# The same decoder layer, its instruction order made by the scheduler's timeline model instead of its default model

## The chip, the cores and the metric

The kernel runs on one core of one Trainium2 chip. A core has five engines that work at the same time, each from a queue of its own that it takes strictly in the order in which it was written: TensorE (PE in the profile; its weight loads are shown apart as PEld), VectorE (DVE), ScalarE (ACT), GpSimd (POOL) and SyncE (SP, which in this kernel issues nearly all the DMA transfers). An instruction that needs another engine's result waits for a semaphore, and everything behind it in its queue waits too. Data lies in a memory of 128 partitions that all engines reach (SBUF), and matmul sums in a small accumulator memory (PSUM). The metric is device microseconds (us) of one execution of the whole program.

## What is computed

One inference step of one decoder layer, for a prompt of 1024 tokens and eight samples of 8 tokens each (1088 tokens), with 1024 features, all in 32-bit floats.

```python
def decoder_layer(x, ...):
    x = x + 0.5 * rms_norm(swiglu_ffn(rms_norm(x, ffn1_norm_pre), ffn1_w_up, ffn1_w_down), ffn1_norm_post)
    m, ... = parallel_mixers(rms_norm(x, mix_norm_pre), w_in, ...)
    x = x + rms_norm(m, mix_norm_post)
    x = x + 0.5 * rms_norm(swiglu_ffn(rms_norm(x, ffn2_norm_pre), ffn2_w_up, ffn2_w_down), ffn2_norm_post)
    return x, ...

def parallel_mixers(h, ...):
    qa, ka, va, qkvb, zb, ab, bb, ga, gb = split_columns(h @ w_in)
    oa, ... = swa_prompt(qa, ka, va, attn_sinks)        # or swa_sample with a cache: window of 128
    xb, ... = causal_short_conv(qkvb, conv_buf, conv_w)
    ...
    ob, new_s = gated_delta_chunked(qb, kb, vb, g, beta, s0)
    ob = rms_norm(ob, dn_out_norm) * jax.nn.silu(zb)
    merged = jax.nn.sigmoid(ga) * (oa @ w_branch_a) + jax.nn.sigmoid(gb) * (ob @ w_branch_b)
    return merged @ w_out, ...

def step(s, xs):                                        # the delta net's scan over chunks, per head
    v_new = v_u_n - einsum(k_cum_n, s)
    o = einsum(q_dec_n, s) + einsum(qk_n, v_new)
    s = s * g_tot_n + einsum(k_dec_n, v_new)
    return s, o
```

A feed-forward block (FFN) has an inner width of 2816, that is 22 blocks of 128 gate and 128 up columns. The delta net has 4 heads; each solves a triangular system within its chunks and then runs the scan above.

## The kernel before

**Precision and weights.** A weight block is loaded by SyncE, split by ScalarE into a rounded high part (L111) and by VectorE into the low remainder (L112), and each product is three matmuls: high by high, high by low, low by high (`gemm`, L138 to L140; in the FFN's combined products L462 to L464; in its down projection L343 to L345). Tokens stand in three chunks of 384, 384 and 320 columns.

**Stages, in the order in which they are written.** First FFN (`FFN.run`): the third chunk takes its first groups of blocks (`pass_a`), then the first two chunks together by a scheme of seven products instead of eight (`two`, on sums and differences that `combine` makes, L264 to L272), then the rest of the third chunk. Norms (`rms`: squares on ScalarE, additions on VectorE at L168 and L171, a column sum by TensorE at L175) and residuals (`post`) are generators whose steps are handed out between the products. Then the mixers: projections for keys, values and queries (`do_kv`, `do_q`), the attention over the prompt and the samples, and for each of the four delta net heads the convolution projections (`conv_head`), a gate projection (`z_unit`) and `delta_head`, with the 16 gate projections (`gate_unit`, `gate_do`) written between and behind them. Then the two branch products (`br`), the output projection, and the second FFN in the manner of the first.

**`delta_head`** is a chain of small matmuls and VectorE and ScalarE steps: the norms of q and k (L1001), decay matrices and Gram products in two groups of four chunks (L1060 to L1087), the inverse of the diagonal 32x32 blocks with a round trip through DRAM (L1143 to L1155), the rest of the inverse (L1174 to L1198), the scan over eight chunks (L1217 to L1236), the samples' part (L1246 to L1270), and the output norm. Heads 0 and 2 use one set of buffers and the PSUM tag `ph`, heads 1 and 3 another set and `py`. The output goes to DRAM (`obd`) and is loaded and split again for the branch products.

**What sets the order.** The functions above only say what depends on what. When the block that holds the context closes, the tile library's scheduler plays the program through on a model of the machine. Whenever an engine of the model can take an instruction, it gives it the one of the highest priority among those whose inputs and buffers are ready there; priority is the order of writing, moved forward where the kernel says `high_priority(offset=...)`. The order that comes out is written into the engines' queues, with semaphores for the dependences, and the chip follows it. The kernel steers this by hand in a few places: the splits of weights and the evacuations of projections are moved forward by 20000 places (L110, L682 and others), column sums of two norms are kept behind two products that are ready (`behind`, L718), and the attention's matmuls of the two halves are chained in turn. Three PSUM banks (`pa`) take the products, two each `ph` and `py`, one `po` the norms; eight slots hold split weights (`wp`).

**Lines that the prediction speaks of**: L171 and L175 (a norm's last addition and its column sum), L198 (the first scaling of the input), L272 (the low part of a combination), L468 (adding a PSUM sum to an SBUF tile in `two`), L111 and L112 (weight splits), L176 (the reciprocal root behind a norm's sum), L1008, L1063, L1174, L1217 and L1001 in `delta_head`, and the branch products' matmuls (`oabh`, `h_br`).

## Time and profile before

| | us |
|---|---|
| median of three runs | 2462.98 |
| lowest and highest of them | 2456.78, 2473.88 |
| the profiled execution | 2454.17 |
| span from its first to its last instruction | 2452.4 |
| ACT busy in it | 1146.2 |
| mean granted TensorE clock | 0.991 |

The profile gives for each engine its busy time, and for each instruction what ended the idle time before it. In it L12 is line 12 of the kernel, and `out<-in` names the tiles written and read. A table of stretches gives for each stretch its length, then for each engine its busy time and number of instructions, then the granted clock as a share of the full one, the share of time the DMA engines were busy, and GB/s. The list of waits gives the total, the number and the longest. A matmul's record lasts longer than the time to the next start, since matmuls are pipelined, so busy time is not time at full rate.

The order of time of the main stages, by the lines seen in the trace: the first FFN from 6 to some 775 us, the mixers to some 1490, the branch and output projections to some 1680, the second FFN to the end.

### The profile page before, as it was taken

How to read it: one execution, taken by the hardware profiler on the slowest of the kernel's cores; microseconds unless marked ns; L12 is line 12 of the kernel's file. 1: busy time of each engine (PE TensorE's matmuls, PEld its weight loads, DVE VectorE, ACT ScalarE, POOL GpSimd, SP SyncE). 2: the span in 40 equal slices, each digit the busy share in tenths (PEclk: the TensorE clock that was granted, in tenths of full speed). 3: DMA queues.
4: the chain of work that ended last, by engine and by line, in shares of the span. 5: the costliest groups of instructions: out<-in, count | busy, mean ns of one | idle time of the engine just before them, and what ended most of it. 6: DMA issues, size and time to landing. Idle time of an engine off the chain costs nothing.

```text
span 2452.4 us, 39218 instructions
## 1 busy us (share of the span) xinstructions
PE 2396.3 (98%) x14654; PEld 2307.2 (94%) x14654; DVE 1752.0 (71%) x3550; ACT 1146.2 (47%) x2326; POOL 48.6 (2%) x36
## 2 busy tenths in 40 slices
PE   8999999999999999999999999999999999999997
PEld 7999999999998988798898889999999999999997
DVE  8887657757788577698796646655997576676677
ACT  7644423324465377644655333255754333233344
POOL 0000000000000000000101000000000000000000
PEclk9999999999999999999999999999999999999998
DMA  7332212213454301222222345435523122122453
GB/s 269 125 112 86 74 48 86 70 52 112 155 175 142 105 29 45 77 65 73 71 68 73 99 143 158 142 129 184 182 93 97 48 82 78 45 85 80 152 164 133
DMA packets 159759, 257.98 MB, mean 105 GB/s; under 512 B 34800, under 2 KB 65968, under 8 KB 159560
## 3 DMA queue, kind: packets, MB, share of 16 engines
q1 hardware_dynamic: 159568, 255.47, 32.4%
q8 instruction: 115, 1.88, 0.3%
q14 instruction: 76, 0.62, 0.1%
HBM read 219.43 MB, written 36.96 MB: 105 GB/s over the span
## 4 chain that ended last, share of the span: by engine, by line
PE 43%; DVE 6%; DMA 2%; ACT 1%; issue 1%; SPq 0%; DVEq 0%; ACTq 0%
PE pa L139 6%; PE pa L140 6%; PE pa L138 6%; PE pa L462 4%; PE pa L463 4%; PE pa L464 4%; PE py L344 2%; PE py L345 2%; PE ph L345 2%; PE ph L344 2%; PE ph L343 2%; PE py L343 2%; DMA q_c_a<-in_up_dram 1%; DVE s L1149 1%; DVE s L1143 1%
## 5 line engine op out<-in xcount | busy, mean ns | idle before, releaser
L463 PE MATMUL pa<-cl,h_c_s 128*128 128x384 f32 x704 | 236.4, 336 | 4.7 <-DVE cl L272 4.7
L462 PE MATMUL pa<-ch,h_c_s 128*128 128x384 f32 x704 | 237.4, 337 | 2.0 <-DVE t L468 1.4
L464 PE MATMUL pa<-ch,l_c_s 128*128 128x384 f32 x704 | 236.2, 336 | 0.0
L468 DVE TENSOR_TENSOR t<-pa,t 128x384 f32<-128x384 f32 x308 | 170.3, 554 | 83.6 <-PE pa L464 83.1
L462 PE MATMUL pa<-ch,h_c_a 128*128 128x384 f32 x528 | 176.8, 335 | 0.1
L464 PE MATMUL pa<-ch,l_c_a 128*128 128x384 f32 x528 | 176.6, 334 | 0.0
L463 PE MATMUL pa<-cl,h_c_a 128*128 128x384 f32 x528 | 176.5, 334 | 0.0
L111 ACT CAST h_c_a<-r_c_a 128x512 fp32r<-128x512 f32 x132 | 81.8, 619 | 129.8 <-PE pa L463 110.9
L462 PEld LDWEIGHTS pa<-ch,h_c_s 128*128 128x128 f32 x704 | 132.8, 189 | 5.6 <-DVE t L468 5.2
L463 PEld LDWEIGHTS pa<-cl,h_c_s 128*128 128x128 f32 x704 | 133.0, 189 | 4.9 <-DVE cl L272 4.9
L464 PEld LDWEIGHTS pa<-ch,l_c_s 128*128 128x128 f32 x704 | 132.9, 189 | 0.0
L111 ACT CAST h_c_s<-q_c_s 128x512 fp32r<-128x512 f32 x132 | 82.0, 621 | 107.1 <-PE pa L463 96.3
L139 PE MATMUL pa<-xbl,h_ga 128*128 128x384 f32 (+1 forms) x384 | 129.3, 337 | 0.0
L138 PE MATMUL pa<-xbh,h_ga 128*128 128x384 f32 (+1 forms) x384 | 128.7, 335 | 0.0
L140 PE MATMUL pa<-xbh,l_ga 128*128 128x384 f32 (+1 forms) x384 | 128.4, 334 | 0.0
L462 PEld LDWEIGHTS pa<-ch,h_c_a 128*128 128x128 f32 x528 | 99.1, 188 | 0.8 <-DVE t L468 0.6
L463 PEld LDWEIGHTS pa<-cl,h_c_a 128*128 128x128 f32 x528 | 99.1, 188 | 0.0
L464 PEld LDWEIGHTS pa<-ch,l_c_a 128*128 128x128 f32 x528 | 99.1, 188 | 0.0
L138 PE MATMUL pa<-xbh,h_qkv 128*128 128x384 f32 (+1 forms) x288 | 96.7, 336 | 0.0
L139 PE MATMUL pa<-xbl,h_qkv 128*128 128x384 f32 (+1 forms) x288 | 96.6, 335 | 0.0
L140 PE MATMUL pa<-xbh,l_qkv 128*128 128x384 f32 (+1 forms) x288 | 96.3, 334 | 0.0
L111 ACT CAST h_c_s<-r_c_s 128x512 fp32r<-128x512 f32 x44 | 27.4, 623 | 146.4 <-PE pa L463 130.6
(603 smaller groups left out, 7438.4 us busy)
## 6 DMA issues: line engine op xcount, KB each, us to landing
r_c_a<-in_up_dram SPq DMA_DIRECT2D x132, 256.0 KB
q_c_a<-in_up_dram SPq DMA_DIRECT2D x44, 256.0 KB
q_ub<-in_up_dram SPq DMA_DIRECT2D x44, 256.0 KB
r_ub<-in_up_dram SPq DMA_DIRECT2D x44, 256.0 KB
r_ua<-in_up_dram SPq DMA_DIRECT2D x42, 256.0 KB
q_ua<-in_up_dram SPq DMA_DIRECT2D x42, 256.0 KB
r_da<-in_dn_dram SPq DMA_DIRECT2D x40, 256.0 KB
q_da<-in_dn_dram SPq DMA_DIRECT2D x40, 256.0 KB
```

The lines of the kernel that those rows point to most:

```text
L111: nc.scalar.copy(hi, full)
L138: nc.tensor.matmul(ps[:, :n], hi[:, j, :], at(xh, k), start=first, stop=False)
L139: nc.tensor.matmul(ps[:, :n], hi[:, j, :], at(xl, k), start=False, stop=False)
L140: mm = nc.tensor.matmul(ps[:, :n], lo[:, j, :], at(xh, k), start=False, stop=last)
L343: nc.tensor.matmul(ps[:, :n], hi[:, i, :], hh, start=i == 0, stop=False)
L344: nc.tensor.matmul(ps[:, :n], hi[:, i, :], hl, start=False, stop=False)
L345: nc.tensor.matmul(ps[:, :n], lo[:, i, :], hh, start=False, stop=i == len(hs) - 1)
L462: nc.tensor.matmul(ps, wh[:, k, :], xh[:, k, :], start=k == 0, stop=False)
L463: nc.tensor.matmul(ps, wh[:, k, :], xl[:, k, :], start=False, stop=False)
L464: nc.tensor.matmul(ps, wl[:, k, :], xh[:, k, :], start=False, stop=k == 3)
L468: nc.vector.tensor_tensor(out=out, in0=ps, in1=other, op=ALU.add)
L1143: nc.vector.tensor_tensor(out=tv, in0=Md[:, j + 1 :, j : j + 1].to_broadcast([34, m, j + 1]), in1=Ld[:, j : j + 1, 0 : j + 1].to_broadcast ...
```

## The change

The context that schedules the program is made with one more argument:

```diff
-    with _tile.TileContext(nc) as tc:
+    with _tile.TileContext(nc, schedule_with_timeline_sim=True) as tc:
         body(tc, d)
```

With it the scheduler plays the program through on another model of the machine: a timeline on which every instruction is a sequence of steps (decoding, waiting, holding an engine, taking effect, telling others), with queues of bounded length in front of the engines and a model of TensorE's clock. The default model has its own durations and no such steps. The rule by which an instruction is chosen, the priorities, the dependences laid by hand, the tiles and the instructions themselves are the same in both. What differs is at which moment of the model an engine is free and an input is ready, and so which instruction is chosen, and so the order within each engine's queue.

## The prediction

> **What bounds the kernel now.** I read the page's busy times first, then a table of the span cut into seven stages, then the list of what TensorE waited for, then the order of time around its longest waits.
>
> ```profile
> span 2452.4 us, 39218 instructions
> PE 2396.3 (98%) x14654; PEld 2307.2 (94%) x14654; DVE 1752.0 (71%) x3550; ACT 1146.2 (47%) x2326; POOL 48.6 (2%) x36
> ```
> ```profile
> core 0: us, PE busy (x) PEld busy (x) DVE busy (x) ACT busy (x) POOL busy (x), PEclk, DMA share, GB/s
> 0.00:100.00 100.00, 90.34 (x573) 85.96 (x574) 82.25 (x151) 74.27 (x150) 0.20 (x4) 1.00 0.65 221
> 100.00:700.00 600.00, 599.00 (x3522) 596.52 (x3521) 428.87 (x751) 240.29 (x450) 0.00 (x0) 1.00 0.29 92
> 700.00:1500.00 800.00, 778.52 (x4972) 702.64 (x4971) 579.60 (x1482) 432.45 (x970) 48.42 (x32) 0.99 0.29 91
> 1500.00:1700.00 200.00, 200.00 (x1230) 199.12 (x1230) 110.92 (x199) 78.79 (x154) 0.00 (x0) 1.00 0.41 134
> 1700.00:1900.00 200.00, 192.63 (x1197) 190.18 (x1197) 176.36 (x295) 114.16 (x223) 0.00 (x0) 0.98 0.42 139
> 1900.00:2400.00 500.00, 499.58 (x2935) 498.04 (x2935) 336.66 (x599) 187.80 (x347) 0.00 (x0) 1.00 0.30 96
> 2400.00:2452.40 52.40, 36.21 (x237) 34.74 (x235) 37.37 (x77) 18.40 (x36) 0.00 (x0) 0.86 0.29 102
> ```
>
> TensorE is the bound: it is busy for 2396.3 of 2452.4 us, and its 14654 matmuls stay what they are. A new order can touch only the 56.1 us in which it is idle, time that a busy record hides, and the clock. By stage the idle time is 9.66 us at the start, 1.00 in the first feed-forward block, 21.48 in the mixers (700 to 1500), 0 and 7.37 around the entry to the second feed-forward block, 0.42 in its body and 16.19 at the end. The two long feed-forward stages have nothing to win and a great deal to lose; the mixers and the entry at 1800 are where an order was badly guessed.
>
> ```profile
> PE po L175 <- DVE rms L171: 8.7, 4, 3.6
> PE pa L138 <- ACT xuh L198: 6.0, 1, 6.0
> PE pa L463 <- DVE cl L272: 4.7, 1, 4.7
> ...
> PE py L1174 <- DMA s<-bd: 2.1, 1, 2.1
> ```
> ```profile
> 774.08 0.33 PE L139 MATMUL pa<-xbl,h_k 128*128 128x384 f32 x1
> 774.25 0.34 PE L140 MATMUL pa<-xbh,l_k 128*128 128x384 f32 x1
> 777.56 0.91 PE L175 MATMUL po<-rms,eye 128*128 128x384 f32 x2 [2.97 <-DVE rms L171]
> ...
> 781.29 0.69 PE L138 MATMUL pa<-xbh,h_kvq 128*128 128x384 f32 x1
> ```
>
> The second fence is the kind of thing that a better model should mend. The column sums of the norm (L175) were placed in TensorE's stream ahead of the query projections (L138, h_kvq), as if the norm's additions on VectorE were done by then. They came 2.97 us late, and products that don't need that norm's sums stood behind them in the queue.
>
> ```profile
> 1018.00:1027.80 9.80, 6.08 (x49) 4.97 (x48) 8.67 (x24) 4.61 (x12) 2.55 (x2) 1.00 0.15 40
> ...
> 1341.90:1345.30 3.40, 3.40 (x26) 3.10 (x25) 1.67 (x6) 0.61 (x4) 1.16 (x1) 1.00 0.23 72
> 1798.00:1806.10 8.10, 5.21 (x34) 4.91 (x32) 8.10 (x10) 6.02 (x15) 0.00 (x0) 1.00 0.26 72
> ```
> ```profile
> 778.70:785.50 6.80, 5.86 (x16) 4.42 (x17) 4.53 (x10) 2.58 (x6) 0.00 (x0) 0.50 0.06 21
> 1027.80:1034.70 6.90, 6.90 (x24) 5.30 (x23) 3.97 (x11) 2.68 (x6) 0.39 (x2) 0.51 0.14 20
> 1178.00:1181.40 3.40, 3.40 (x13) 3.40 (x12) 1.46 (x10) 3.36 (x4) 0.00 (x0) 0.50 0.06 8
> 1345.30:1348.70 3.40, 3.40 (x11) 2.46 (x9) 2.62 (x7) 1.29 (x2) 0.74 (x1) 0.50 0.73 240
> 1806.10:1812.90 6.80, 5.02 (x16) 5.02 (x17) 5.69 (x8) 3.09 (x7) 0.00 (x0) 0.50 0.06 24
> ```
>
> These are two tables of short stretches, with the columns of the stage table; the last column but two is the granted clock. After each thin stretch of TensorE the clock is 0.50 for 3.4 to 6.9 us, so a gap is paid twice. TensorE is busy for 24.58 us of these five stretches (5.86 + 6.90 + 3.40 + 3.40 + 5.02); at full clock that work takes half, so 12.3 us are lost.
>
> **The change, part by part.** No instruction is added or removed: 14654 matmuls, 3550 VectorE, 2326 ScalarE and 36 GpSimd operations, and all DMAs stay, with their buffers and dependences. What moves is the place of each of them in its engine's queue, SyncE's DMA issues and GpSimd's included.
>
> *What an order could win at most.* Idle time in the mixers and the entry at 1800 is 21.48 + 7.37 = 28.9 us; with the clock's 12.3 that is 41.1 us. The start isn't counted: its 9.66 us hold the 6.0 us before the first matmul, while the first transfers land. Nor is the end: the last norm is a chain with no other work left.
>
> *What of it a better order can reach.* Two stretches have VectorE itself full: 8.10 of 8.10 us before 1806 and 8.67 of 9.80 before 1028. There TensorE's idle time (4.7 us in front of L463, and 9.80 - 6.08 = 3.72 us in the other) and half of the slow clock behind it ((5.02 + 6.90) / 2 = 5.96) are VectorE's work, 14.4 us that I leave. The other 26.7 us are latencies that ready products could cover. I take three quarters of them, 20 us, since transfers such as the 2.1 us in front of L1174 will still be guessed wrongly in places.
>
> [...]
>
> *What a new order can cost.* Three prices, each from both sides. (a) Evacuations on VectorE:
>
> ```profile
> L468 DVE TENSOR_TENSOR t<-pa,t 128x384 f32<-128x384 f32 x308 | 170.3, 554 | 83.6 <-PE pa L464 83.1
> ```
>
> Sums of the feed-forward blocks are taken out of three PSUM banks by L468 in 0.554 us each. VectorE waits 83.1 us for TensorE there, and TensorE is idle for 1.00 and 0.42 us in the two long stages, so the banks cover the delay now. A product is 12 matmuls, 0.17 us apart (774.08 and 774.25 above are two starts), some 2.1 us; two further banks cover two products, 4.2 us, less the 0.554 itself. An evacuation placed more than about 3.6 us late costs time. At best this gives back those 1.4 us; at worst one product's time (2.1 us) is lost in each of the 44 blocks, 92 us. I take nothing, as VectorE is busy for 428.87 of 600 us there. (b) The order of transfers: only 2.1 us of TensorE's waits end on one; bounds -2.1 and a few times that; I take nothing. (c) ScalarE's table loads:
>
> ```profile
> L176 ACT ACT_TABLE_LOAD x13 | 16.7, 1283 | 0.2
> ```
>
> An order that alternates functions more often pays 1.283 us of ScalarE each. ScalarE is busy for 432.45 of 800 us in the mixers, which covers it except in a norm's chain; taken as nothing, with 13 at most either way (16.7 us) as the bound.
>
> *Sum.* 2454.17 us is the profiled execution (2452.4 of span and 1.8 around it); less 20 it is 2434. It lies 8.8 us under the median of the runs shown, 2462.98 us, so on that footing I expect **2443 us**, 0.8% less.
>
> **The rivals.** *All of it goes:* also VectorE's share, 41 us, 2422 us. For it speaks that the order of VectorE's own three 1.75 us pieces before L463 is free; against it, that these 8.10 us were full.
>
> *Nothing net:* new waits of the same size come instead, 2463 us. For it: the feed-forward stages and 1500 to 1700, 1300 us together, have 1.4 us of idle time, so the present order is already good. An order that comes out nearly the same belongs here.
>
> *Slower, by the delta net's chain.*
>
> ```profile
> 1016.94 1.16 PE L1063 MATMUL ph<-s,s 128*128 128x128 f32 x8 [0.55 <-DVE s L1008]
> ...
> 1437.09 2.31 PE py L1001 x6
> ...
> L138 PEld LDWEIGHTS pa<-oabh,h_br x192: 187/188/188, 1488.4 to 1582.7; 128*128 128x128 f32 x192
> ```
> ```profile
> 1410.72 0.49 PE L1217 MATMUL py<-s,s 128*128 128x128 f32 x2
> ...
> 1412.85 0.47 PE L1217 MATMUL py<-s,s 128*128 128x128 f32 x2
> ```
>
> The four heads run from 1017 to 1439 us as one dependent chain, with projections put between its steps. The branch products (h_br) need the last head and start at 1488.4. In the 49 us between, that output is stored, loaded and split: 24 pieces (by the code, three chunks of eight) of some 0.55 us on VectorE, as in L468's row, are 13 us, and two transfers of a little over the 2.1 us of L1174's wait make some 19. So the chain may grow by about 30 us, 7% of its 422, before TensorE runs out of projections. One chunk step takes 2.1 us (two starts of L1217) and holds two hops. If the new model puts three more matmuls of 0.17 us (0.52 us) ahead of each hop, a head with some 36 hops (16 in its chunk loop, about 20 by the code) grows by 19 us, four by 75, and 45 us are exposed: 2508 us. Each further matmul per hop adds 25 us. Against it: a model whose times are right puts a chain step in as soon as its input is there.
>
> **How the numbers follow.** About 1% (24.6 us) is what a measurement of this kernel can tell from no change: faster is under 2438, slower over 2488. Most waits shrink: 0.42, of which 0.22 under 2438 (own range 2425 to 2458). All of it goes: 0.12, faster. Nothing net: 0.18, same. The chain is exposed: 0.28, slower. So faster 0.34, same 0.38, slower 0.28. The range runs from 2418, just past the case of all 41 us, to 2520, which takes in one chain case of 45 us and leaves the worse ones, about 0.12, out.
>
> **What would show it.** Right: no wait of some 3 us before L175 near 780; idle time of the 700 to 1500 stage near 8 us instead of 21.5; slow-clock stretches only behind VectorE-full windows; 1900 to 2400 as full as now. Wrong: TensorE waiting on L468 in the feed-forward stages; a last head that ends later than 1470 with TensorE idle before h_br; many more table loads than 13 in L176; a start or an end that is longer than 9.66 and 16.19 us of idle time.

## The result and the profile after

| | before | after |
|---|---|---|
| median, us | 2459.98 | 2531.99 |
| lowest and highest, us | 2456.78, 2473.88 | 2526.56, 2535.47 |
| profiled execution and its span, us | 2454.17, 2452.4 | 2532.87, 2531.2 |
| mean granted TensorE clock | 0.991 | 0.972 |

The medians are of four runs each; a fourth run of the kernel before moved its median from the 2462.98 us shown above. The change makes the kernel slower: the ratio of the times is 1.028, with a 95% interval from 1.0235 to 1.0325. The table of stages of the changed kernel, with the columns that it had before:

```profile
core 0: us, PE busy (x) PEld busy (x) DVE busy (x) ACT busy (x) POOL busy (x), PEclk, DMA share, GB/s
0.00:100.00 100.00, 83.15 (x515) 78.93 (x516) 74.95 (x141) 69.97 (x140) 0.20 (x4) 0.97 0.62 207
100.00:700.00 600.00, 600.00 (x3541) 599.73 (x3540) 428.41 (x752) 240.80 (x449) 0.00 (x0) 1.00 0.30 93
700.00:1500.00 800.00, 740.27 (x4655) 675.98 (x4655) 543.90 (x1412) 399.84 (x905) 41.29 (x28) 0.95 0.24 75
1500.00:1700.00 200.00, 185.29 (x1076) 174.07 (x1075) 114.11 (x203) 73.69 (x144) 9.88 (x4) 0.92 0.48 152
1700.00:1900.00 200.00, 197.15 (x1237) 194.27 (x1236) 146.05 (x246) 113.59 (x230) 0.00 (x0) 0.99 0.42 141
1900.00:2400.00 500.00, 500.00 (x2886) 500.00 (x2885) 347.63 (x622) 187.13 (x347) 0.00 (x0) 1.00 0.27 84
2400.00:2531.20 131.20, 114.94 (x756) 113.20 (x754) 93.51 (x179) 57.93 (x110) 0.00 (x0) 0.94 0.46 157
```

The span is 78.8 us longer. TensorE's idle time went from 56.1 to 110.4 us (+54.3). Its busy time went from 2396.28 to 2420.80 us (+24.5) for the same 14654 matmuls, at a mean clock of 0.972 instead of 0.991. The two make the 78.8 us.

By stage, idle time from 700 to 1700 went from 21.48 to 59.73 + 14.71 = 74.4 us (+53.0). The first 100 us have 7.2 more. The stretch at 1700 to 1900 has 4.5 less, and the two long feed-forward stages have none left. From its first matmul to the end the second feed-forward block took 2452.4 - 1679.4 = 773.0 us before and 2531.2 - 1766.0 = 765.2 after. So the loss lies in the mixers and at the entry to the branch products that follow them, and one gain of some 8 us lies behind them.

Within the mixers, three stretches of TensorE stand out (same columns):

```profile
1004.00:1043.00 39.00, 23.30 (x157) 13.92 (x155) 18.24 (x53) 25.91 (x57) 0.00 (x0) 0.72 0.23 81
...
1184.00:1240.00 56.00, 45.35 (x261) 36.03 (x261) 22.88 (x63) 22.73 (x59) 2.90 (x2) 0.74 0.14 39
...
1540.00:1580.00 40.00, 27.02 (x86) 19.79 (x87) 17.68 (x27) 12.84 (x24) 4.84 (x3) 0.62 0.51 164
```

They are idle for 15.7, 10.7 and 13.0 us, at clocks of 0.72, 0.74 and 0.62. In each of them the chain runs with hardly a projection between its steps: at the end of attention, where heads 0 and 1 run their chunk loops side by side, and at the end of head 3 with the entry to the branch products. The instruction rows of the heads' first matmul, the last gate product, and the chain's end with the entry to the branch products in time order:

```profile
L1063 PEld LDWEIGHTS ph<-s,s x32: 186/192/338, 1042.9 to 1294.7; 128*128 128x128 f32 x32
```
```profile
L139 PE MATMUL pa<-xbl,h_ga x384: 302/334/740, 1091.5 to 1536.7; 128*128 128x384 f32 x128, 128*128 128x320 f32 x64
```
```profile
1557.03 3.67 PE L1001 MATMUL py<-s,eye 128*128 128x512 f32 x6
1565.48 0.69 PE L138 MATMUL pa<-oabh,h_br 128*128 128x384 f32 x1 [4.78 <-ACT oabh L191]
1569.58 0.69 PE L139 MATMUL pa<-oabl,h_br 128*128 128x384 f32 x1 [3.42 <-DVE oabl L192]
```

The heads start at 1042.9 instead of 1017 (+26) and end at 1560.7 instead of 1439.4 (+121), so their 422 us have become 518. The gates are used up at 1536.7, 24 us before the chain ends; before the change they lasted for 49 us behind it. The branch products start 77 us later (1565.5 instead of 1488.5). Of the 121 us, then, 44 went into the cover that was there, and 77 show. At their entry TensorE waits again, for the pieces of `oab`, and the second feed-forward block starts 1766.0 - 1679.4 = 86.6 us later, so the branch and output products lose a further 9.6 us.

How a step gets later can be read in the chunk loop, here from one product of L1217 to the next step of the chain, L1224; first head 3 before the change, then head 2 after it (start, duration, operation):

```profile
1410.97 0.40 PE L139 MATMUL pa<-xbl,h_ga 128*128 128x320 f32 x1
...
1411.78 0.34 PE L138 MATMUL pa<-xbh,h_ga 128*128 128x384 f32 x1
1411.95 0.49 PE L1224 MATMUL py<-s,s 128*128 128x128 f32 x2
```
```profile
1437.70 0.49 PE L1217 MATMUL ph<-s,s 128*128 128x128 f32 x2
1437.94 0.42 PE L140 MATMUL pa<-xbh,l_ga 128*128 128x384 f32 x1
...
1441.58 0.31 PE L139 MATMUL pa<-xbl,h_ga 128*128 128x320 f32 x1
1441.73 0.38 PE L1224 MATMUL ph<-s,s 128*128 128x128 f32 x2
```

Before, 6 gate matmuls stand between them and the hop takes 1.2 us; after, 24 do and it takes 4.0. What L1224 waits for last is ScalarE's copy, whose rows in the two cases are:

```profile
1411.63 0.27 ACT L1223 COPY s<-py 128x128 f32<-128x128 f32 x1 [0.58 <-DVE s L1221]
```
```profile
1438.61 0.27 ACT L1223 COPY s<-ph 128x128 f32<-128x128 f32 x1 [0.58 <-DVE s L1221]
```

Before, L1224 starts 0.05 us after the copy's end; after, 2.85 us, all of them filled with gate matmuls. Over the 32 steps of the four chunk loops the time from the copy's end to L1224 went from 0.05 to 1.55 us at the median, while the other two lags of the step stayed under 0.1 us (from TensorE to VectorE, and from VectorE to ScalarE). The waits in front of L1174, which needs a head's blocks, grew as well, from 2.1 us (the engine's tile, what it waits for, us in total, times, longest):

```profile
PE ph L1174 <- DMA s<-bd: 9.1, 2, 5.6
PE py L1174 <- DMA s<-bd: 6.9, 2, 5.2
```

In the written order of TensorE's queue the runs of projections between other work of the mixers went from 4 to 13 matmuls at the median.

### The profile page after: what moved, and what is told of

It is laid out like the page before. It is cut to its first block, busy times and chain, and to the rows that moved or that the text cites. A ratio compares the mean times of both kernels' runs of the same rounds, so it can differ in the third digit from the quotient of the medians.

```text
span 2531.2 us, 39119 instructions
## 1 busy us (share of the span) xinstructions
PE 2420.8 (96%) x14654; PEld 2336.2 (92%) x14654; DVE 1748.6 (69%) x3550; ACT 1142.9 (45%) x2324; POOL 51.4 (2%) x36
## 4 chain that ended last, share of the span: by engine, by line
PE 84%; DVE 7%; DMA 3%; ACT 2%; issue 1%; SPq 0%; DVEq 0%; ACTq 0%
PE pa L139 10%; PE pa L138 10%; PE pa L140 10%; PE pa L462 8%; PE pa L464 8%; PE pa L463 8%; PE ph L343 3%; PE py L345 3%; PE ph L344 3%; PE py L343 3%; PE py L344 3%; PE ph L345 3%; DMA bd<-s 1%; DMA s<-bd 1%; DVE t L965 1%
## 5 line engine op out<-in xcount | busy, mean ns | idle before, releaser
L462 PE MATMUL pa<-ch,h_c_s 128*128 128x384 f32 x704 | 235.7, 335 | 0.0
L463 PE MATMUL pa<-cl,h_c_s 128*128 128x384 f32 x704 | 235.3, 334 | 0.0
L468 DVE TENSOR_TENSOR t<-pa,t 128x384 f32<-128x384 f32 x308 | 166.5, 552 | 82.2 <-PE pa L464 80.8
L462 PE MATMUL pa<-ch,h_c_a 128*128 128x384 f32 x528 | 177.1, 335 | 1.8 <-ACT t L380 1.8
L463 PE MATMUL pa<-cl,h_c_a 128*128 128x384 f32 x528 | 177.1, 335 | 0.0
L462 PEld LDWEIGHTS pa<-ch,h_c_s 128*128 128x128 f32 x704 | 132.3, 188 | 0.1
L463 PEld LDWEIGHTS pa<-cl,h_c_s 128*128 128x128 f32 x704 | 132.2, 188 | 0.0
L138 PE MATMUL pa<-xbh,h_ga 128*128 128x384 f32 (+1 forms) x384 | 129.4, 337 | 0.1
L140 PE MATMUL pa<-xbh,l_ga 128*128 128x384 f32 (+1 forms) x384 | 128.2, 334 | 0.0
L462 PEld LDWEIGHTS pa<-ch,h_c_a 128*128 128x128 f32 x528 | 99.4, 188 | 2.0 <-ACT t L380 2.0
L463 PEld LDWEIGHTS pa<-cl,h_c_a 128*128 128x128 f32 x528 | 99.5, 188 | 0.0
L140 PE MATMUL pa<-xbh,l_qkv 128*128 128x384 f32 (+1 forms) x288 | 96.6, 335 | 0.0
L138 PE MATMUL pa<-xbh,h_qkv 128*128 128x384 f32 (+1 forms) x288 | 95.9, 333 | 0.0
L112 DVE TENSOR_TENSOR l_c_s<-q_c_s,h_c_s 128x512 fp32r<-128x512 f32 x132 | 90.5, 687 | 0.3 <-ACT h_c_s L111 0.2
```

The costliest lines, as they stand in the source:

```text
L112: nc.vector.tensor_tensor(out=lo, in0=full, in1=f32(hi), op=ALU.subtract)
L138: nc.tensor.matmul(ps[:, :n], hi[:, j, :], at(xh, k), start=first, stop=False)
L140: mm = nc.tensor.matmul(ps[:, :n], lo[:, j, :], at(xh, k), start=False, stop=last)
L462: nc.tensor.matmul(ps, wh[:, k, :], xh[:, k, :], start=k == 0, stop=False)
L463: nc.tensor.matmul(ps, wh[:, k, :], xl[:, k, :], start=False, stop=False)
L468: nc.vector.tensor_tensor(out=out, in0=ps, in1=other, op=ALU.add)
```

## The experiments

The runs are called e1 to e18, and stand here by the question that they answer. Most of them hold one or more engines to the order that the other model gave them, by edges that only order, within the mixers (from L631 to the end of the gates). Both orders are made from the same program:

```diff
+    order = trace(BASE, None)[2]
+    nc, feed, _ = trace(FLAG, order)
...
+        for name, eng in order:
...
+            if eng.split(".")[1] in PIN[stage]:
+                if eng in last:
+                    tc.add_manual_dep(ins[k], last[eng], dep, reason="the other model's order")
+                last[eng] = name
```

In all of them the work is the same. The kernel before, timed beside them, had medians from 2458.05 to 2460.23 us.

### One engine's order at a time

```diff
+BASE, FLAG, PIN = False, True, ((), ('PE',), (), ())
```


> The timeline model makes the order, but within the mixers (from the sum at 631 to the end of the delta net) TensorE alone is held to the order that the default model gave it; VectorE, ScalarE, SyncE and GpSimd are free. Theory A, TensorE's order is the cause (it puts runs of 13 projection matmuls, at the median, between two steps of a chain instead of 4, the chain gets longer and the projections run out): the mixers get back nearly all of their 79 us; heads 0 to 3 take 420 to 440 us instead of 517; about 2455 us. Theory B, the order on VectorE and ScalarE stretches the chain: heads stay above 490 us; 2510 to 2535. Theory C, the order of transfers on SyncE (the waits in front of L1174 grew from 2.1 to 16 us): as B.

e1: 2498.74 us, ratio 1.0154 (1.0126 to 1.0183): 33 of the 72 us come back, between what A and B expected. The heads take some 465 us. The first row of TensorE's waits, and the rows of head 2's substitution loop on VectorE (count, shortest/median/longest in ns, first and last start), before and in this run:

```profile
PE ph L1174 <- DMA s<-bd: 21.7, 2, 19.9
```
```profile
L1143 DVE TENSOR_TENSOR s<-s,s x31: 169/356/2337, 1242.3 to 1288.9; 34x31 f32<-34x31 f32 x2, 34x60 f32<-34x60 f32 x2, 34x87 f32<-34x87 f32 x2, 34x112 f32<-34x112 f32 x2
```
```profile
L1143 DVE TENSOR_TENSOR s<-s,s x31: 183/366/2091, 1269.4 to 1337.3; 34x31 f32<-34x31 f32 x2, 34x60 f32<-34x60 f32 x2, 34x87 f32<-34x87 f32 x2, 34x112 f32<-34x112 f32 x2
```

L1174 waits for the blocks that this loop makes, by way of a transfer. The loop's 62 dependent operations take 22 us by themselves in both; the loop lasts 47.3 us before and 68.3 here, as 121 other operations (55.2 us, their records overlapping in part) stand between its steps instead of 92 (36.8 us); the counts of 135 and 106 in the expectation of e15 take in waits on semaphores. VectorE does to this chain what TensorE does to the other.

```diff
+BASE, FLAG, PIN = True, False, ((), ('PE',), (), ())
```


> The reverse: the default model makes the order, but TensorE is held in the mixers to the order that the timeline model gave it. Theory A: the loss appears, heads take about 515 us and the time is 2460 + 77 = about 2537 us. Theory B (VectorE and ScalarE) and C (transfers): 2455 to 2480, heads below 450 us.

e2: 2555.98 us, ratio 1.0398 (1.0365 to 1.0432): 24 us more than the change itself. TensorE's order is enough for the loss. That the other engines don't fit it is one reading of the further 24 us; e7 below, where they do, still takes 2548.55 us, so most of it isn't explained.

```diff
+BASE, FLAG, PIN = False, True, ((), ('DVE', 'Activation'), (), ())
```


> The timeline model makes the order, but VectorE and ScalarE are held in the mixers to the default model's order; TensorE's order is the timeline model's own, given those. Theory A: no gain, 2520 to 2550 us, since TensorE still takes projections in long runs. Theory B: the mixers get their 79 us back, about 2455 us. Theory C: about 2530.

e3: 2593.82 us in a single run, worse than all others and outside every expectation. TensorE, in the timeline model's own order for these fixed ones, takes projections in runs of 20 at the median. Theory B falls. It doesn't show that these two orders are harmless, since they fit another order of TensorE.

```diff
+BASE, FLAG, PIN = False, True, ((), ('PE', 'SP'), (), ())
```


> As e1, but TensorE and SyncE's transfers are held in the mixers to the default model's order, VectorE and ScalarE are free. Theory A2: within 10 us of the 2499 us with TensorE alone. Theory C: 2455 to 2470 us, the heads back to 425 us.

e6: 2540.69 us, ratio 1.0337 (1.0316 to 1.0358): 42 us worse than e1, not better. TensorE waits 43.0 us at L1174 and 11.0 us for the cache of keys (L910). Theory C falls, and A2's time is missed too. My reading, which no run separates, is that a transfer held to an old place waits for work that now comes later.

### Engines together

```diff
+BASE, FLAG, PIN = False, True, ((), ('PE', 'DVE', 'Activation'), (), ())
```


> As e1, but in the mixers TensorE, VectorE and ScalarE are all held to the default model's order; the transfers on SyncE and GpSimd's work stay in the timeline model's order. Held on TensorE alone, the heads took 465 us and the run 2499 us. Theory A2, the loss belongs to the orders of the three compute engines together (one that fits the other): heads near 425 us, 2450 to 2465 us (the first block's 8 us more and the second's 8 less cancel). Theory C, the other half is the order of the transfers: it stays within 10 us of 2499.

e5: 2457.13 us, ratio 0.9994 (0.9982 to 1.0005). The whole loss is gone, with the transfers in the timeline model's order. The row of the mixers' stage is nearly that of before (778.52 busy, clock 0.99):

```profile
700.00:1500.00 800.00, 777.07 (x4988) 702.26 (x4987) 579.03 (x1489) 436.32 (x979) 49.19 (x32) 0.99 0.29 92
```

The reverse in the default model's run:

```diff
+BASE, FLAG, PIN = True, False, ((), ('PE', 'DVE', 'Activation'), (), ())
```


> As e2 (2556 us, 18 more than the loss it was to reproduce), but the default model's run is held in the mixers to the timeline model's order on TensorE, VectorE and ScalarE. Theory A2: the timeline model's loss without the misfit between the engines, 2460 + 79 = about 2539 us, heads near 517 us. Theory C: below 2510, since the transfers go in the default order.

e7: 2548.55 us in a single run; the heads take 522 us. These three orders make the whole loss, and some 10 us more than A2 expected, with the transfers in the default order.

```diff
+BASE, FLAG, PIN = False, True, ((), ('PE', 'DVE'), (), ())
```


> As e1 (TensorE held in the mixers to the default order: 2499 us, with a wait of 19.9 us in front of L1174 for a head's blocks, whose substitution loop on VectorE took 68.3 us instead of 47.3), with VectorE held too; ScalarE free. Theory V, the other half of the loss is VectorE's order: the loop is back near 47 us, the wait near 2, and the time within 8 us of the 2457 us that all three engines gave. Theory S, it is ScalarE's: 2485 to 2500 us.

e16: 2473.45 us, ratio 1.0051 (1.0034 to 1.0069). The loop and the wait (2.5 us at most) came out as V expected, the time didn't: it is 16 us above the run with all three engines, where 8 were allowed. Head 2's loop is back:

```profile
L1143 DVE TENSOR_TENSOR s<-s,s x31: 179/358/2342, 1255.9 to 1303.8; 34x31 f32<-34x31 f32 x2, 34x60 f32<-34x60 f32 x2, 34x87 f32<-34x87 f32 x2, 34x112 f32<-34x112 f32 x2
```

```diff
+BASE, FLAG, PIN = False, True, ((), ('PE', 'Activation'), (), ())
```


> As e1, with ScalarE held too; VectorE free. Theory V: 2485 to 2500 us, the loop of head 2 above 60 us. Theory S: 2450 to 2465 us.

e17: 2496.52 us, ratio 1.0153 (1.013 to 1.0176), with the loop at 67.9 us and a wait of 18.1 us at L1174. So of the mixers' loss TensorE's order gives back 33 us and VectorE's 25 more; ScalarE's gives 16 once both are right and 2 when VectorE's is not. The shares depend on the order in which they are taken: with ScalarE's in place, VectorE's gives 39.

### Which part of the mixers

The same edges, in a part of their own that begins with the first head's convolution:

```diff
+    attention_sample(); MARK.append(len(list(nc.cur_bb.bb.instructions)))
+BASE, FLAG, PIN = False, True, ((), (), ('PE', 'DVE', 'Activation'), (), ())
```

> The timeline model, with TensorE, VectorE and ScalarE held to the default model's order from the first head's convolution to the end of the gates; attention, and what stands before it, in the timeline model's order. Theory A2: attention and the start of the heads keep their 26 us (1017 to 1043), the heads' and the overrun's 51 us come back: 2475 to 2490 us. If attention's delay is only a consequence of what the heads' projections do: 2455 to 2465.

e11: 2475.29 us, ratio 1.0061 (1.0039 to 1.0084), as A2 expected. The heads start at 1042.7 us and take 431 us. Heads and gates are 57 of the 75 us between the change and e5, attention and what stands before it the other 18.

### Is it a choice, and is it the projections' place?

```diff
-    attention_prompt()
+    with tc.high_priority(offset=10000): attention_prompt()
```
(and so for `attention_sample` and the four calls of `delta_head`)

> The timeline model, with a priority over the projections for all of attention and of the four heads. Theory A, with runs of projections that are taken while no step of the chain is ready by the model's times: a priority decides only between instructions that are ready at the same moment, so the runs stay (median 12 or 13 matmuls) and so does the time, 2515 to 2545 us. Rival D, the model has both ready and chooses the projections: the runs fall to about 4 and the time to 2450 to 2470.

e8: 2527.55 us in a single run, runs of 12 at the median. A priority hardly changes anything, which speaks for a model that takes a projection where it has no step of the chain ready.

```diff
+        if name not in FILL:
+            step = name
+        elif step and step != last and at[step] < at[name]:
+            tc.add_manual_dep(ins[at[name]], step, dep, reason="no earlier than in the default order")
```


> The timeline model, with one rule: in attention and the heads no projection matmul may stand ahead of the chain step that it stood behind in the default model's order; chain steps and all other engines are free. Theory A, projections spent too early are TensorE's part of the loss: most of the 33 us that the whole TensorE order gave back in e1 come back, 2495 to 2508 us. If it was the order of the chain steps among themselves: 2522 or more.

e14: 2514.74 us, ratio 1.0224 (1.0199 to 1.0249): 17 us, half of what the whole order of TensorE gave and between the two expectations. The heads take 480 us instead of 518, and 252 gate matmuls are left behind the last step, so the cover is kept. But from 700 to 1500 us TensorE is idle for 64.8 us (59.7 in the changed kernel): with the projections held back, the waits of the chain are bare. Projections spent too early are thus not the whole of TensorE's part.

```diff
+        j == 0 and turns and tc.add_manual_dep(st.ins, turns[-1], NOSYNC, reason="heads in turn")
```


> The timeline model, with one rule: on VectorE the first step of a head's substitution loop (62 dependent operations, L1143 and L1149) stands behind the last of the head before. In the timeline model's run heads 0 and 1 share VectorE step by step, 1083.4 to 1178.3 us for both, where the default order finished head 0's at 1095.5 and head 1's at 1155.3; both heads then reach TensorE together and the projections that need a head's buffers aren't there. Theory G, this sharing is a cause of its own: head 0's loop takes 40 to 52 us and ends by 1140, its chunk loop starts some 30 us earlier than 1183.7, TensorE's idle time of 10.7 us at 1184 to 1240 and the half clock there go, 2500 to 2518 us. Theory H, only TensorE's runs of projections matter: 2525 to 2540.

e13: 2524.72 us, ratio 1.0267 (1.0237 to 1.0296), outside both ranges by a little. The expectation misread the trace: the one stretch of 94.9 us for both heads was taken for a step-by-step sharing. Row by row, head 0's loop ends near 1143 and head 1's begins at 1137, so only four steps of each overlap. The 7 us lie at the edge of the runs' spread. Theory G falls with its premise: there was hardly any sharing to undo, so what sharing would cost isn't shown.

Both edits together:

> Both rules of e13 and e14. Theories A and G together: the two gains add for the most part, 2465 to 2485 us. If the wait of 20 us in front of L1174 that e1 kept comes from other work on VectorE between the substitution's steps (135 operations for 55.6 us in head 2's loop in e1, 106 for 37.4 before) and not from the sharing: 2490 to 2505.

e15: 2513.22 us, ratio 1.0219 (1.0193 to 1.0244): nothing beyond e14, and outside both ranges. Head 2's loop takes 68.3 us as in e1, so the wait that e1 kept isn't a matter of sharing.

### Longer runs put into the default order

The default model's run, with TensorE held in the mixers to its own order, in which each run of gates between two steps of heads 2 and 3 is filled up to 12, or 16:

```diff
+RUN, LEAD = 12, 600
+            while own and n in LATE and run < RUN and taken < min(passed + LEAD, len(todo)):
+                out.append(todo[taken])
+                taken, run = taken + 1, run + 1
```


> The default model's order, in which, in heads 2 and 3 alone, each place between two chain steps that holds gate projections (1 to 9 matmuls for the most part) gets at least 12 of them, taken from those that come later. Behind the last chain step 89 gate matmuls are left where there were 301, so 212 have moved ahead of chain steps, at 49.0 us / 301 = 0.163 us each 35 us. Theory E, a longer run costs only when the projections run out before the chain ends: the last head ends 35 us later, near 1474, and the time doesn't change, 2455 to 2463 us, since 89 x 0.163 = 14.5 us of gates are left over. Theory F, each delay of the chain is paid in full: 2458 + 35 = 2493 us.

e9: 2491.3 us, ratio 1.0126 (1.0103 to 1.0149). It is F's time but not F's reason: the last head ends at 1498.9, 59.5 us later and not 35. Two places in the order of time carry it:

```profile
1416.14 2.05 PE L1174 MATMUL py<-s,s 128*128 128x128 f32 x8 [14.16 <-DMA s<-bd]
...
1517.32 0.69 PE L138 MATMUL pa<-oabh,h_br 128*128 128x384 f32 x1 [5.36 <-ACT oabh L191]
```

Between heads 2 and 3 the default order has a run of 229 gates, which covers head 3's substitution loop. Here 32 are left there: TensorE waits 14.2 us, and the granted clock over 1390 to 1440 us is 0.83 (1.00 before), as much as some 17 of these 50 us at half clock would make. E counted what is left at the end and not what each wait in the middle needs. The clock is also 0.96 over 1240 to 1290 us (1.00 before), behind the first runs that were filled up, at the start of head 2 (12 gates at 1170.1 us where 4 stood, then 12 at 1203.0 and at 1207.5 where 2 stood). There the run is already 12.5 us late: a stretch of 181 projections starts at 1250.4 instead of 1237.9.

```diff
-RUN, LEAD = 12, 600
+RUN, LEAD = 16, 2000
```


> As e9 with at least 16. All 301 gate matmuls now stand ahead of chain steps and the last 14 lines of the chain (from the seventh product of L1217 on) have none between them. Theory E: the last head ends 49 us later plus what the bare end takes, and TensorE is idle between its steps and until the branch products: about 10 us of bare steps and 5 us of entry, 2468 to 2478 us. Theory F: 2458 + 49 + 10 = 2517 us or more.

e10: 2505.52 us, ratio 1.0184 (1.0161 to 1.0208), between E and F. The gates are gone at 1499.6 and the chain ends at 1515.9. So longer runs, in two heads, make a loss in the default order, and it grows with their length: 33 and 47 us. VectorE and ScalarE were free to follow TensorE's new order, and how much of the loss lies in theirs wasn't separated.

### The gain in the second feed-forward block

The default order, with the timeline model's in this block alone: for all three compute engines, for VectorE and ScalarE, and for TensorE.

```diff
+BASE, FLAG, PIN = True, False, ((), (), (), ('PE', 'DVE', 'Activation'))
```


> The default model makes the order up to the second feed-forward block; in that block TensorE, VectorE and ScalarE are held to the timeline model's order. From its first matmul to the end that block took 773.0 us before and 765.2 after, with the 4.7 us wait in front of L463 gone. If that gain comes from the order inside the block: about 2452 us, 8 less than before. If it came from what precedes the block (the later start leaves its inputs ready): no change, 2460.

e4: 2452.7 us, ratio 0.9971 (0.9957 to 0.9986), the fastest version: 5.5 us under the kernel before, with the block at 767.5 us and no wait in front of L463.

```diff
+BASE, FLAG, PIN = True, False, ((), (), (), ('DVE', 'Activation'))
```


> As e4 (ratio 0.9971), but only VectorE and ScalarE are held to the timeline model's order in the second feed-forward block; TensorE goes by the default model. If the 4.7 us in front of L463 were a matter of when VectorE makes its pieces: ratio 0.996 to 0.999, as e4. If TensorE's own order of products gave the gain: 0.999 to 1.002.

e12: 2456.86 us, ratio 0.999 (0.9976 to 1.0004), where the two ranges meet; L463 still waits 4.2 us.

```diff
+BASE, FLAG, PIN = True, False, ((), (), (), ('PE',))
```


> As e4 (ratio 0.9971) and e12 (VectorE and ScalarE alone: 0.9990, the 4.7 us in front of L463 unchanged), with TensorE alone held to the timeline model's order in the second feed-forward block. If the gain is TensorE's order of products: 0.996 to 0.999, and the wait in front of L463 gone. If all three are needed: 0.999 to 1.002.

e18: 2464.06 us, ratio 1.0018 (1.0003 to 1.0033). The wait in front of L463 is gone, as the first reading expected, but others stand in its place (4.8 us in front of L343, 3.4 in front of L462), and the time is that of the second. Neither part alone gave the gain; TensorE with only one of the other two wasn't run.

## Why the prediction was wrong, step by step

- **The bound** (TensorE, with idle time and slow clock as the only things an order can change) holds: both terms together are the 78.8 us.
- **The gain of 20 us** failed at "latencies that ready products could cover". It took for granted that a better match of work to waits was what the other model would make. In the mixers it made a worse one: idle time rose from 21.48 to 59.73 us in the stage where it was to fall to some 8.
- **What was left to VectorE** was the part that came: the 4.7 us in front of L463 were called VectorE's own, since it was full in that stretch. They went with another order of all three engines (e4), and the block is 5.5 us shorter there, some 8 in the changed kernel. With TensorE's order alone (e18) they went too, but other waits took their place.
- **(a) Evacuations at nothing** held: no wait for L468 is among the changed kernel's waits, and the two long stages have no idle time. **(b) Transfers at nothing** was wrong in size: L1174 waits 16.0 us instead of 2.1, more than the bound of a few times that. It is not the order of transfers that makes it, since e5 leaves that order as it is and the waits are back at 2.4 and 1.6 us; by e1 and e16 what L1174 waits for is late on VectorE. **(c) Table loads** held, 12 in L176 instead of 13.
- **The rival of the delta net's chain** is what happened. The step that failed is the sentence against it, "a model whose times are right puts a chain step in as soon as its input is there". On the chip the input was there, 2.85 us early in the case shown, and 24 gate matmuls were in the queue ahead of it; a priority (e8) didn't help. Why the model's steps become ready so late isn't shown by these runs.
- **Its size**, 2508 us for 2532. Three matmuls more per hop were taken; in the chunk loops there are 6.4 more (9.6 at the mean instead of 3.2). The heads grew by 95 us and not by 75, though at its price of 25 us for each further matmul per hop 6.4 would have given some 160. That heads run side by side from 1184 to 1240 may be why; no run separates it. The cover was 44 us and not 30. It left out attention, at whose end the heads start 26 us late, and VectorE's queue, where 25 us of the loss lie (e16 against e1). It also left out the branch and output products, which lose 9.6 us. With the measured terms, from one profiled execution to the other: 2454.2 + 95 + 26 - 44 + 9.6, less the 8 of the last block, is 2533, where 2532.87 was measured.
- **The signs**: L175 has no wait of 3 us near 780 any more, but TensorE waits 2.8 us there for L683 instead; 1900 to 2400 is full, and nothing waits on L468; but the last head ended at 1561 with TensorE idle before h_br, which was named as the sign of being wrong, and the start has 16.85 us of idle time instead of 9.66.

## What to carry to other kernels

Where independent products fill the waits of a dependent chain, count them as a stock: how many matmuls each wait of the chain needs, and how many are left behind its last step. An order that spends them in long runs pays twice, once as a later step and once as a bare wait where they are missing. Holding them back is not enough by itself: that gave 17 us. An order belongs to all engines at once: with TensorE's part of the good order 33 of 75 us came back, with the transfers' part added it got worse, and with three engines' parts all was back.

## What the runs showed of the hardware

The granted clock fell to half behind stretches that differ in how busy TensorE was. Two pairs of stretches of the changed kernel (columns of the stage table), and the longest gap before the first pair's slow part:

```profile
1079.00:1085.70 6.70, 3.86 (x17) 2.55 (x16) 2.73 (x11) 1.59 (x4) 0.00 (x0) 1.00 0.07 22
1085.70:1089.10 3.40, 3.40 (x15) 3.40 (x14) 3.09 (x14) 1.81 (x5) 0.00 (x0) 0.50 0.18 63
...
1212.00:1218.80 6.80, 6.80 (x54) 6.33 (x54) 2.39 (x7) 2.42 (x10) 0.65 (x1) 1.00 0.04 12
1218.80:1232.40 13.60, 13.09 (x30) 6.77 (x30) 5.53 (x14) 3.42 (x8) 1.25 (x1) 0.50 0.25 80
```
```profile
1085.06 0.42 PE L138 MATMUL pa<-xbh,h_z 128*128 128x320 f32 x1 [2.84 <-DVE t L1018]
```

From 1212 to 1218.8 it is busy for 6.80 of 6.80 us with small matmuls of the chain (54 of them, most 128x128), and runs at 0.50 for the next 13.6 us; before 1085.7 it is busy for 3.86 of 6.70 us, with 2.84 us as its longest gap, and 3.4 us at 0.50 follow. In the same trace 3.49 us of idle time end at 1389.63 us, and the clock is 0.50 for the 3.4 us from 1389.5. In the kernel before, the 3.40 us at 0.50 from 1345.30 follow 3.40 us that are all busy, so "after each thin stretch" doesn't hold for all five of the prediction's stretches. At 0.50 the 128x320 matmuls of L138 to L140 start 0.27 us apart (1085.81 to 1088.74 us), at 1.00 they start 0.15 us apart (1089.19 to 1089.48). What the granted clock goes by isn't shown; in this kernel, of 20.4 us of chained matmuls with no projections between them (1212 to 1232.4 us), 13.6 were paid at half clock.
